# Retention outputs copied out of PSUM at once, and a planner that counts series of narrow matmuls

## The chip, the cores and the metric

The kernel runs on one core of one Trainium2 chip. The metric is the device time of one execution in microseconds (us); the kernel before is given by the median of three runs. Profiles are of single executions.

## The reference

The program is a two-layer decoder trunk on 1024 positions of width 1024, all in float32. Layer 0 is a retention layer with 4 heads (query/key width 256, value width 512), layer 1 a stick-breaking attention with 8 heads. The change touches the retention layer's output and the order of the whole program. Cut to what matters:

```python
u = rms_norm(h, ret_norm_pre); proj = u @ ret_w_in            # q, k, v, g
q, k = rope(q), rope(k) * 256 ** -0.5
o = retention_chunkwise(q, k, v)                              # per head: (q k^T * decay) v + state
mu  = mean(o, axis=-1); var = mean((o - mu) ** 2, axis=-1)    # over a head's 512 values
o = (o - mu) * rsqrt(var + EPS)                               # normalise each row of each head
o = merge_heads(o) * silu(g)
y = o @ ret_w_out; h = h + rms_norm(y, ret_norm_post)
... # shared K/V from h, then layer 1: stick-breaking attention with its own q and gate
A[t,s] = sigmoid(z_ts) * prod_{s<j<t} (1 - sigmoid(z_tj));  o = A v;  y = (o * silu(g)) @ sb_w_out
h = h + rms_norm(y, sb_norm_post)
```

## The kernel before

**How the work is tiled.** Positions come in two halves of 512, each in blocks of 128 (one block is the 128 partitions). Every float32 product is made of three matmuls, since each operand is kept as a high and a low part (`split`: ScalarE (ACT) copies the source rounded to the matmul's type, then VectorE (DVE) subtracts it from the source for the low part). A matmul with 512 moving columns is called wide here; one with 384, 256 or 128 columns, and every 128x128 transpose by an identity matrix, is narrow. The large projections (weights `wraw`/`raw` loaded from memory, split into `whl`; input parts `xh`, `qk`, `oT`, `op`) use two-by-two block products with seven instead of eight block multiplications, so sums of weight blocks are formed on DVE first. They accumulate in the PSUM banks `pma` and `pmb` (two each), and in part in `pz` and `po`.

**Stages.** First the retention layer's projections (to about 430 us). Then, spread between further projections, the eight retention units (4 heads by 2 halves, about 430 to 690 us): scores in `pz` (two banks), outputs in `po` (two banks). Then the first output projection, normalisation and the second layer's projections, the stick-breaking heads (about 1100 to 1500 us: score rows in `pz`, a scan on DVE, transposes of the weights `A` into `pz`, split into `AT`, products into `po`), and the last projection.

**One retention block.** `o(ib)` in `AHead.mix` computes a block's 128x512 output in a `po` bank. DVE takes its mean and variance from the bank (`bn_stats`, `bn_aggr`, and the negated mean `nm`), GpSimd (POOL) adds epsilon, raises to the power -1/2 and multiplies (`r`, `nb`). One call later `normed()` has ACT read the bank once more, with scale `r` and bias `nb`, into the SBUF tile `on` (a half of a `sgn` buffer); in `gate()` DVE multiplies by the gate `sg` and PE transposes the four 128x128 pieces into `pz`, from where ACT copies them to `on`/`o` for storage. Bank `po` is held until that second reading.

**What sets the order.** All operations are recorded first (`Recorder`), with their dependencies through tiles: a reader depends on the writers of the same cells and a writer on their readers, while two readers do not depend on each other. `Plan` then orders every engine's queue. `Plan.run` walks a clock forward with the costs from `Recorder.cost`: for PE it looks at the next 100 matmuls in program order and takes the one with the lowest sum of lateness (its operand should be ready EARLY = 350 ns ahead), expected waiting (times IDLE = 10) and distance from the front (PLACE = 5 ns each). The other engines take, of what is ready first, what is due first (`Plan.limits`). Ten rounds are made, each with the due times of the last, and each resulting order is tried with random durations (`Plan.trial`, six tosses); the order with the lowest mean is emitted. Loads and stores are issued by SyncE (SP) in an order set the same way. Instructions are recorded at one line of the file (L234, L235 after the change), so the profile tells them apart by tile names: `po<-v,sc` writes a tile `po` from `v` and `sc`.

In this kernel's rope step, which comes up below, DVE forms four products from two PSUM banks and a table (`f<-po,tab`), and POOL adds them in pairs (`f<-f,f`).

Of the kernel before, what the change touches and what calls it, by code (L numbers as in the profile page):

```python
# [45 lines left out]
EARLY, PLACE, IDLE = 350, 5, 10  # L46
# [99 lines left out]
class Recorder:  # L146
# [39 lines left out]
    def cost(self, o, out, ins):  # L186
# [9 lines left out]
        if e == PEE:  # L196
            fp = ins[0].tile.dt == F32 and m == "transpose"
            if m == "transpose":
                pace = 111 if fp else 58 + (0 if self.turning else 142)
            else:  # L200
                pace = max(13.3 + n / 2.4, 112) + (2 if n == 512 else 0)
            self.turning = m == "transpose" and not fp
            o.step, o.took = pace, pace + 162
            return
# [82 lines left out]
class Plan:  # L287
# [39 lines left out]
    def run(self, late, look=True):  # L327
# [16 lines left out]
        since = {}  # L344
# [20 lines left out]
        def best(e):  # L365
            if e == PEE:
                c = None
                for k, i in enumerate(pe[:PE_AHEAD]):
                    if c and k * PLACE >= c[0]:
                        break  # L370
                    if need[i]:
                        continue
                    r = possible(i)
                    if r is None:
                        continue
                    x = max(r if r > ready[i] else 0.0, given[i])
                    wait = max(r - free[e], 0.0)
                    x = max(x + EARLY - free[e], 0.0) + wait * IDLE + k * PLACE
                    if c is None or x < c[0]:
                        c = (x, free[e] + wait, i)  # L380
# [20 lines left out]
        while len(order) < n:  # L401
# [13 lines left out]
            else:  # L415
                took = o.took
                if o.port:
# [32 lines left out]
    def trial(self, order, seed):  # L450
# [3 lines left out]
        busy, server = {DVEE: 0.0, POOLE: 0.0}, 0.0  # L454
# [3 lines left out]
        for o in order:  # L458
# [14 lines left out]
            elif e == PEE:  # L473
                more = 0 if o.step < 200 or x > 0.16 else 6.5 if x > 0.01 else 90
# [42 lines left out]
def trunk(ctx, tc, xT, wts, gains, trig, ident_in, cols, grow_in, out):  # L517
# [299 lines left out]
    class AHead:  # L817
# [65 lines left out]
        def mix(self):  # L883
# [40 lines left out]
            def o(ib):  # L924
# [10 lines left out]
                for jb in blocks:  # L935
                    n = slice(128 * (ib - jb), 128 * (ib - jb) + 128)
                    sc, v = self.sc[jb], self.v[jb]
                    mm3(p[:], sc[:, 0, n], sc[:, 1, n], v[:, 0, :], v[:, 1, :], not state and jb == first, jb == ib)
                bs, mv = S("small", [6]), S("small", [2])
# [8 lines left out]
                late.append((ib, p, r, nb))  # L948
# [5 lines left out]
            def normed():  # L954
                ib, p, r, nb = late.pop(0)
                if ib % 2 == 0:
                    self.on2 = S("sgn", [1024])
                on = self.on2[:, 512 * (ib % 2):512 * (ib % 2) + 512]
                A_.activation(on, p[:], AF.Identity, scale=r[:], bias=nb[:])
                self.on.append(on)  # L960
# [842 lines left out]
```

## Time and profile before

| what | value |
| --- | --- |
| median of three runs | 1577.93 us (1577.35 to 1577.95) |
| the profiled execution | 1576.62 us, its span 1574.9 us |
| PE busy | 1565.2 us (99%), 7416 matmuls |
| DVE busy | 1304.8 us (83%) |
| ACT busy | 828.3 us (53%) |
| POOL busy | 212.6 us (13%) |
| mean granted TensorE clock | 0.999 |

The profile's page gives busy times by engine, groups of instructions (line, engine, operation, `out<-in` by tile names, shapes, count, busy time, mean duration of one, idle time before them and what ended it), and the chain of work that ended last. The trace also answers with the waits of one engine, with a timeline of one engine in a window (start in us, time covered in us, instruction, count; consecutive instructions of one kind are one row), and with busy times by window. Matmuls overlap in the pipeline, so that a duration of 389 ns goes with a start every 227 ns: pace is read from starts.

### The profile page before, as it was taken

The page shows a single profiled execution, that of the slowest core. Times are in us where ns is not written, and L with a number is a line of the kernel's source. Part 1 is how long each engine was busy: PE and PEld are TensorE (multiplying, and loading weights), DVE is VectorE, ACT ScalarE, POOL GpSimd, SP SyncE. Part 2 cuts the span into 40 slices and gives each one's busy share as a digit, 9 for nine tenths or more (in the row PEclk, how much of TensorE's full clock was granted, in tenths as well). Part 3 has the DMA queues.
Part 4 walks back from the last instruction along what each step waited for, and adds up shares of the span by engine and source line. Part 5 has one row for each costly group of instructions (what it writes and reads, how often), then busy time and mean ns, then how long its engine had stood idle before and what let it go on. Part 6 is the DMA issues. An engine that isn't in the chain of part 4 may idle for free.

```text
span 1574.9 us, 22257 instructions
## 1 busy us (share of the span) xinstructions
PE 1565.2 (99%) x7416; PEld 1305.7 (83%) x7416; DVE 1304.8 (83%) x1909; ACT 828.3 (53%) x1470; POOL 212.6 (13%) x298
## 2 busy tenths in 40 slices
PE   9999999999999999999999999999999999999998
PEld 7888888878888888888888888888888888888886
DVE  7999889797677988999989856748788878777888
ACT  7643432313466765646665545545555655554564
POOL 0100015240022222420000000001120111211100
PEclk9999999999999999999999999999999999999999
DMA  8779887378556897884686969667889768884674
GB/s 293 250 256 333 282 324 236 128 258 291 177 189 215 303 342 272 318 312 164 219 295 239 327 212 348 223 238 260 298 303 347 255 239 298 312 324 156 231 282 170
DMA packets 176946, 414.20 MB, mean 263 GB/s; under 512 B 19904, under 2 KB 20544, under 8 KB 176832
## 3 DMA queue, kind: packets, MB, share of 16 engines
q1 hardware_dynamic: 176688, 412.73, 74.0%
q8 instruction: 58, 0.95, 0.2%
q14 instruction: 56, 0.46, 0.1%
q10 hardware_dynamic: 144, 0.07, 0.0%
HBM read 299.47 MB, written 113.25 MB: 262 GB/s over the span
## 4 chain that ended last, share of the span: by engine, by line
PE 99%; DVE 1%; issue 0%; POOL 0%; ACT 0%; DVEq 0%; ACTq 0%
PE pma L234 29%; PE pmb L234 29%; PE po L234 23%; PE pz L234 19%; POOL col L234 0%; DVE whl L234 0%; DVE wraw L234 0%; DVE f L234 0%; DVE small L234 0%; DVE A L234 0%; DVE S L234 0%; ACT f L234 0%; DVEq L1799 0%; ACT acc L234 0%; ACT AT L234 0%
## 5 line engine op out<-in xcount | busy, mean ns | idle before, releaser
L234 ACT ACTIVATE whl<-wraw 128x512 fp32r<-128x512 f32 (+1 forms) x264 | 157.8, 628 | 240.8 <-DVE wraw L234 69.6
L234 DVE TENSOR_TENSOR whl<-wraw,whl 128x512 fp32r<-128x512 f32 x264 | 187.5, 733 | 77.2 <-ACT whl L234 76.7
L234 PE MATMUL pma<-whl,xh 128*128 128x512 f32 x480 | 126.4, 393 | 1.2 <-DVE whl L234 1.0
L234 PE MATMUL pmb<-whl,xh 128*128 128x512 f32 x480 | 124.3, 390 | 0.0
L234 PE MATMUL pmb<-xh,whl 128*128 128x512 f32 x408 | 105.9, 390 | 0.0
L234 PEld LDWEIGHTS pmb<-whl,xh 128*128 128x128 f32 x480 | 89.6, 188 | 18.6 <-ACT f L234 0.3
L234 PE MATMUL pma<-xh,whl 128*128 128x512 f32 x408 | 105.0, 390 | 0.0
L234 PEld LDWEIGHTS pma<-whl,xh 128*128 128x128 f32 x480 | 88.5, 188 | 19.0 <-DVE whl L234 1.5
L234 PE MATMUL pz<-ko,ko 128*128 128x384 f32 (+3 forms) x480 | 95.8, 323 | 0.0
L234 ACT ACTIVATE AT<-pz 128x512 fp32r<-128x512 f32 (+2 forms) x96 | 44.6, 490 | 97.2 <-PE pz L234 96.0
L234 PE MATMUL pma<-op,whl 128*128 128x512 f32 x336 | 89.8, 396 | 0.0
L234 PEld LDWEIGHTS pmb<-xh,whl 128*128 128x128 f32 x408 | 76.4, 188 | 15.6
L234 PEld LDWEIGHTS pma<-xh,whl 128*128 128x128 f32 x408 | 76.2, 188 | 15.6
L234 POOL TENSOR_TENSOR f<-f,f 128x512 f32<-128x512 f32 x32 | 54.3, 1705 | 249.1 <-DMA raw<-in_wts_dram 153.4
L234 PE MATMUL pmb<-op,whl 128*128 128x512 f32 x336 | 87.6, 391 | 0.0
L234 PEld LDWEIGHTS pz<-ko,ko 128*128 128x128 f32 x480 | 77.8, 189 | 9.4
L234 DVE SCALAR_TENSOR_TENSOR wraw<-wraw,gn,wraw 128x512 f32<-128x512 f32 x96 | 70.7, 747 | 17.7 <-ACT wraw L234 11.8
L234 POOL TENSOR_SCALAR_AFFINE_SELECT f<-f 128x128 f32<-128x128 f32 x64 | 28.9, 469 | 405.5 <-DMA g<-sg 286.6
L234 DVE TENSOR_TENSOR_SCAN sgn<-sgn 128x640 f32<-128x640 f32 (+3 forms) x32 | 61.8, 1932 | 21.8 <-POOL sgn L234 21.7
L234 PE MATMUL pz<-xh,whl 128*128 128x512 f32 x312 | 79.4, 389 | 0.0
L234 PE MATMUL po<-xh,whl 128*128 128x512 f32 x312 | 79.2, 389 | 0.0
L234 DVE TENSOR_TENSOR AT<-pz,AT 128x512 fp32r<-128x512 f32 (+2 forms) x96 | 51.0, 551 | 33.0 <-ACT AT L234 32.9
(220 smaller groups left out, 3682.6 us busy)
## 6 DMA issues: line engine op xcount, KB each, us to landing
wraw<-in_wts_dram SPq DMA_DIRECT2D x431, 256.0 KB, 5.2
raw<-in_wts_dram SPq DMA_DIRECT2D x64, 512.0 KB, 7.1
v<-v SPq DMA_DIRECT2D x64, 512.0 KB, 5.7
ko<-kq SPq DMA_DIRECT2D x40, 512.0 KB, 6.0
raw<-o SPq DMA_DIRECT2D x36, 512.0 KB, 6.6
raw<-oc SPq DMA_DIRECT2D x36, 512.0 KB, 6.6
kq<-v SPq DMA_DIRECT2D x32, 512.0 KB, 6.5
s<-f SPq DMA_DIRECT2D x40, 256.0 KB, 3.4
```

Source lines behind the costliest of these rows:

```text
L234: f(*[_real(a) for a in o.args], **{k: _real(v) for k, v in o.kw.items()})
```

## The change

It has two parts.

1. In `o(ib)` ACT copies the bank into the `sgn` buffer as soon as the block's last matmul is done (`AF.Copy`); `bn_stats` still reads the bank; `normed()` then normalises in place in SBUF. The `sgn` buffer is therefore taken in `o(ib)` instead of in `normed()`.
2. The planner marks narrow PE operations. In `Plan.run` a wide matmul after a narrow one is charged TURN = 300 ns in the choice, so that a series of narrow ones is continued where one is to be had; a narrow one after a wide one moves the plan's clock by SERIES = 40 ns. In `Plan.trial` that charge takes the place of random extra times on wide matmuls; the 2 ns extra for 512 columns in `cost` is dropped.

```diff
--- before.py
+++ after.py
@@ -43,7 +43,7 @@
 DMA_TIME = 4000.0
 PE_AHEAD = 100
 FILL = 15000.0
-EARLY, PLACE, IDLE = 350, 5, 10
+EARLY, PLACE, IDLE, TURN, SERIES = 350, 5, 10, 300, 40
 ROUNDS, TRIALS = 10, 6
 
 
@@ -195,10 +195,11 @@
             return
         if e == PEE:
             fp = ins[0].tile.dt == F32 and m == "transpose"
+            o.narrow = n < 512
             if m == "transpose":
                 pace = 111 if fp else 58 + (0 if self.turning else 142)
             else:
-                pace = max(13.3 + n / 2.4, 112) + (2 if n == 512 else 0)
+                pace = max(13.3 + n / 2.4, 112)
             self.turning = m == "transpose" and not fp
             o.step, o.took = pace, pace + 162
             return
@@ -341,7 +342,7 @@
         ahead = {tag: list(seq) for tag, seq in self.turn.items()}
         left = {t: len(u) for t, u in self.users.items()}
         last = dict.fromkeys(self.users, 0.0)
-        since = {}
+        since, narrow = {}, False
         for o in ops:
             if not need[o.i] and o.engine != PEE:
                 waiting[o.engine].append(o.i)
@@ -375,7 +376,7 @@
                         continue
                     x = max(r if r > ready[i] else 0.0, given[i])
                     wait = max(r - free[e], 0.0)
-                    x = max(x + EARLY - free[e], 0.0) + wait * IDLE + k * PLACE
+                    x = max(x + EARLY - free[e], 0.0) + wait * IDLE + k * PLACE + (TURN if narrow and not ops[i].narrow else 0)
                     if c is None or x < c[0]:
                         c = (x, free[e] + wait, i)
                 return c and c[1:]
@@ -414,6 +415,10 @@
                 free[e] = t + o.step
             else:
                 took = o.took
+                if e == PEE:
+                    if o.narrow and not narrow:
+                        t += SERIES
+                    narrow = o.narrow
                 if o.port:
                     other = POOLE if e == DVEE else DVEE
                     if port[other] > t:
@@ -451,7 +456,7 @@
         toss = random.Random(seed)
         ops = self.ops
         end, after, free = [0.0] * len(ops), [0.0] * len(ops), [0.0] * 5
-        busy, server = {DVEE: 0.0, POOLE: 0.0}, 0.0
+        narrow, busy, server = False, {DVEE: 0.0, POOLE: 0.0}, 0.0
         slots = {tag: [0.0] * seq[0].bufs for tag, seq in self.turn.items()}
         left = {t: len(u) for t, u in self.users.items()}
         since, last = {}, dict.fromkeys(self.users, 0.0)
@@ -471,7 +476,8 @@
                 end[i] = server + (217 if o.store else 717) + toss.expovariate(1 / 250)
                 free[e] = t + 430
             elif e == PEE:
-                more = 0 if o.step < 200 or x > 0.16 else 6.5 if x > 0.01 else 90
+                more = SERIES if o.narrow and not narrow else 0
+                narrow = o.narrow
                 end[i] = t + o.took + more
                 free[e] = t + o.step + more
             else:
@@ -936,6 +942,10 @@
                     n = slice(128 * (ib - jb), 128 * (ib - jb) + 128)
                     sc, v = self.sc[jb], self.v[jb]
                     mm3(p[:], sc[:, 0, n], sc[:, 1, n], v[:, 0, :], v[:, 1, :], not state and jb == first, jb == ib)
+                if ib % 2 == 0:
+                    self.on2 = S("sgn", [1024])
+                on = self.on2[:, 512 * (ib % 2):512 * (ib % 2) + 512]
+                A_.activation(on, p[:], AF.Copy)
                 bs, mv = S("small", [6]), S("small", [2])
                 V.bn_stats(bs[:], p[:])
                 V.bn_aggr(mv[:], bs[:])
@@ -945,18 +955,15 @@
                 G.tensor_tensor(r[:], mv[:, 1:2], cc[:, 16 + 4 * h + ib:17 + 4 * h + ib], ALU.add)
                 G.tensor_tensor(r[:], r[:], mhalf[:, 0:1], ALU.pow)
                 G.tensor_tensor(nb[:], nm[:], r[:], ALU.mult)
-                late.append((ib, p, r, nb))
+                late.append((on, r, nb))
                 if ib:
                     normed()
 
             late = []
 
             def normed():
-                ib, p, r, nb = late.pop(0)
-                if ib % 2 == 0:
-                    self.on2 = S("sgn", [1024])
-                on = self.on2[:, 512 * (ib % 2):512 * (ib % 2) + 512]
-                A_.activation(on, p[:], AF.Identity, scale=r[:], bias=nb[:])
+                on, r, nb = late.pop(0)
+                A_.activation(on, on, AF.Identity, scale=r[:], bias=nb[:])
                 self.on.append(on)
 
             def first():
```

Since the planner orders the whole program, every engine's order changes. Counted in PE's order, the 1192 narrow matmuls and transposes stood in 238 unbroken series, and stand in 168 now. Three places follow.

**DVE near 347 us of the profile before**, where `whl542` (weights of the projection that accumulates in `pma538` to `pmb541`) gets its second low half, the last row. Before:

```order
L234 TENSOR_TENSOR wraw547_3430<-wraw546_3418,wraw547_3430 128x512
L234 TENSOR_TENSOR f2529_3500<-po426_2760,tab228_1408 128x512
L234 TENSOR_TENSOR wraw548_3438<-wraw548_3438,wraw547_3430 128x512
L234 TENSOR_TENSOR f2530_3512<-po427_2765,tab227_1400 128x512
L234 TENSOR_TENSOR wraw551_3458<-wraw550_3446,wraw551_3458 128x512
L234 TENSOR_TENSOR whl542_3456<-wraw548_3438,whl542_3456 128x512
```

Now:

```order
L235 TENSOR_TENSOR wraw547_3431<-wraw546_3419,wraw547_3431 128x512
L235 TENSOR_TENSOR wraw548_3440<-wraw548_3440,wraw547_3431 128x512
L235 TENSOR_TENSOR wraw551_3459<-wraw550_3448,wraw551_3459 128x512
L235 TENSOR_TENSOR whl542_3457<-wraw548_3440,whl542_3457 128x512
L235 TENSOR_TENSOR wraw552_3467<-wraw552_3467,wraw551_3459 128x512
L235 TENSOR_TENSOR f2529_3525<-po426_2756,tab228_1410 128x512
```

The two rope products `f2529` and `f2530` stood ahead of the low half of `whl542` and now stand behind it.

**PE in the stick-breaking stage**, where two tiles of transposed weights (`pz2214`, `pz2217`) are finished and the first of them, split into `AT2215`, is multiplied into `po2222`. Before:

```order
L234 MATMUL pz2214_12188<-ident_68,A2200_12160 128x128
L234 MATMUL pz2217_12191<-ident_68,A2200_12160 128x128
L234 MATMUL pmb2135_11769<-oT1607_8629,whl2208_12148 128x512 x2
L234 MATMUL pmb2136_11775<-oT1607_8629,whl2208_12148 128x512 x2
L234 MATMUL po2222_12245<-AT2215_12234,vo2213_12072 128x512
```

Now:

```order
L235 MATMUL pmb2136_11814<-oT1607_8666,whl2208_12199 128x512 x3
L235 MATMUL pz2214_12215<-ident_68,A2200_12193 128x128
L235 MATMUL pz2217_12221<-ident_68,A2200_12193 128x128
L235 MATMUL po2222_12277<-AT2215_12272,vo2213_12108 128x512
L235 MATMUL po2223_12281<-AT2215_12272,vo2213_12108 128x512
L235 MATMUL pz2220_12285<-ident_68,A2171_12002 128x128
```

Between the end of `pz2214` and the product that needs its split there stood one transpose and four wide matmuls, and now stands one transpose. In another head (`pz2732`, `AT2733`) it is the other way round: there one transpose and one wide matmul stood between them, and now one transpose and four wide matmuls.

**PE in a retention unit**, from a block's last matmuls (`po798` before, `po799` now) to the last transposes of its normalised output (`pz816`). Before:

```order
L234 MATMUL po798_4739<-v762_4617,sc2739_4570 128x512 x3
L234 MATMUL pz807_4773<-ident_68,sgn784_4661 128x128 x4
L234 MATMUL pz808_4780<-ko741_4407,ko745_4425 128x256 x3
L234 MATMUL pz808_4780<-ko743_4413,ko747_4436 128x256 x3
...
L234 MATMUL pz815_4834<-ident_68,sgn805_4742 128x128 x4
L234 MATMUL pma830_4840<-whl797_4321,qk143_1035 128x512 x3
L234 MATMUL pma831_4847<-whl797_4321,qk143_1035 128x512
L234 MATMUL pz816_4851<-ident_68,sgn805_4742 128x128 x4
```

Now:

```order
L235 MATMUL po799_4747<-v762_4598,sc2739_4587 128x512 x3
L235 MATMUL pz807_4780<-ident_68,sgn765_4607 128x128 x4
L235 MATMUL pz808_4788<-ko741_4414,ko745_4435 128x256 x3
L235 MATMUL pz808_4788<-ko743_4422,ko747_4466 128x256 x3
...
L235 MATMUL pz815_4841<-ident_68,sgn787_4719 128x128 x4
L235 MATMUL pma830_4848<-whl798_4332,qk143_1036 128x512 x3
L235 MATMUL pz816_4854<-ident_68,sgn787_4719 128x128 x4
```

(In the gap marked "..." stand 12 wide matmuls and the 4 transposes of `pz814` in both.) One wide matmul fewer stands between the block's end and its last transposes. In DVE's order of the changed program the statistics of 29 of the 32 blocks wait for ACT's copy of the same bank, and in the other 3 the copy waits for the statistics: the framework that builds the program puts the two readings of one bank one after the other, which the planner's dependencies don't hold. With the waits shown, DVE has for this block:

```order
L235 BN_STATS small801_4784<-po799_4747 128x6 [waits Activation_49]
L235 BN_AGGR small802_4795<-small801_4784 128x2 [waits DVE_49]
```

and before:

```order
L234 BN_STATS small800_4776<-po798_4739 128x6 [waits PE_49]
```

Here the wait is for ACT instead of for PE.

## The prediction

> **What bounds the kernel now.** I read the page's busy times and chain first, then PE's own waits, then PE's timeline at the places that those waits name.
>
> ```profile
> PE 1565.2 (99%) x7416; PEld 1305.7 (83%) x7416; DVE 1304.8 (83%) x1909; ACT 828.3 (53%) x1470; POOL 212.6 (13%) x298
> PE 99%; DVE 1%; issue 0%; POOL 0%; ACT 0%; DVEq 0%; ACTq 0%
> ```
>
> PE is the bound from end to end: 99% of the span is its work, and 99% of the chain that ended last. The number of matmuls does not change. So the change can only take away time in which PE stands still or goes slower than it could, and it can only cost what makes PE wait. PE's waits, all of them:
>
> ```profile
> PE pz L234 <- DVE onesr L234: 1.4, 1, 1.4
> PE pma L234 <- DVE whl L234: 1.0, 1, 1.0
> PE po L234 <- ACT AT L234: 0.3, 1, 0.3
> PE pz L234 <- POOL col L234: 0.2, 1, 0.2
> ```
>
> The first is the program's start. None of the others is a wait for a `po` bank: the bank that the first part of the change frees earlier was never missed. What can be won is the second and third wait, and small change. (A wait in this list is only the gap after the pipeline has run dry; the time lost is read from starts below.)
>
> **The pace, and what a series costs.** The first term rests on PE's timeline (start, time covered, instruction, count):
>
> ```profile
> 471.78 1.52 PE L234 MATMUL pmb<-whl,xh 128*128 128x512 f32 x6
> 473.14 1.52 PE L234 MATMUL po<-ko,ko 128*128 128x512 f32 x6
> ...
> 480.43 1.03 PE L234 MATMUL pz<-ident,sgn 128*128 128x128 f32 x8
> 481.22 1.17 PE L234 MATMUL pma<-whl,qk 128*128 128x512 f32 x4
> 482.23 0.60 PE L234 MATMUL pz<-ident,sgn 128*128 128x128 f32 x4
> ...
> 1482.68 0.38 PE L234 MATMUL pz<-ident,A 128*128 128x128 f32 x2
> 1482.82 1.17 PE L234 MATMUL pmb<-whl,op 128*128 128x512 f32 x4
> 1483.83 0.38 PE L234 MATMUL pz<-ident,A 128*128 128x128 f32 x2
> ```
>
> Six wide matmuls take 473.14 - 471.78 = 1.36, so 0.2267 each. From 480.43 to 482.23 are 8 transposes and 4 wide matmuls, 1.80; from 1482.68 to 1483.83 are 2 and 4, 1.15. The difference gives 0.65 / 6 = 0.108 for a transpose, and 1.15 - 0.907 - 0.217 = 0.026 is left for going into a series and out again. Starts are given to 0.01 and a wide matmul is sometimes a few ns late, so a series costs between 0 and 0.04; I take 0.02, below the reading because it holds such lateness too. The orders have 238 and 168 series: 70 fewer x 0.02 = **-1.4 us** (0 to -2.8).
>
> **The wait near 349 us.** Four engines around it, PE first, then DVE, ACT, POOL:
>
> ```profile
> 347.93 0.61 PE L234 MATMUL pz<-whl,qk 128*128 128x512 f32 x2
> 348.68 0.72 PE L234 MATMUL pma<-whl,xh 128*128 128x512 f32 x2
> 349.25 0.63 PE L234 MATMUL pmb<-whl,xh 128*128 128x512 f32 x2
> 350.90 1.19 PE L234 MATMUL pma<-whl,xh 128*128 128x512 f32 x4 [1.03 <-DVE whl L234]
> 351.93 1.07 PE L234 MATMUL pmb<-whl,xh 128*128 128x512 f32 x4
> ```
>
> ```profile
> 346.68 0.69 DVE L234 TENSOR_TENSOR f<-po,tab 128x512 f32<-128x512 f32 x1
> 347.28 0.68 DVE L234 TENSOR_TENSOR wraw<-wraw,wraw 128x512 f32<-128x512 f32 x1
> 347.88 0.68 DVE L234 TENSOR_TENSOR f<-po,tab 128x512 f32<-128x512 f32 x1
> 348.48 0.68 DVE L234 TENSOR_TENSOR wraw<-wraw,wraw 128x512 f32<-128x512 f32 x1
> 349.08 1.77 DVE L234 TENSOR_TENSOR whl<-wraw,whl 128x512 fp32r<-128x512 f32 x1
> ...
> 348.00 0.63 ACT L234 ACTIVATE whl<-wraw 128x512 fp32r<-128x512 f32 x1 [0.57 <-DVE wraw L234]
> ...
> 348.69 1.60 POOL L234 TENSOR_TENSOR f<-f,f 128x512 f32<-128x512 f32 x1 [6.93 <-ACT whl L234]
> ```
>
> From 347.93 to 351.93 are 4.00 us for 10 wide matmuls, which need 2.27: 1.73 lost. PE first wants the high half (ACT, done 348.63), then the low one (DVE, done 350.85, stretched from 0.68 to 1.77 while POOL works until 350.29). In the new order the two `f<-po,tab` stand behind. Then the second sum starts at 346.68 instead of 347.28, ACT's copy runs from 347.40 to 348.03, and the low half from about 348.07 to 348.75; POOL's step waits for one of the moved products and begins after it. Without its first wait (0.30) PE asks for the high half at 348.38 and, four matmuls on, for the low one near 349.29. Both are there, with 0.35 and 0.5 to spare: **-1.7 us** (0 if that margin is eaten by a later start of DVE, which a moved transfer could bring).
>
> **The wait near 1485 us goes, and comes back elsewhere.**
>
> ```profile
> 1483.96 0.48 PE L234 MATMUL pmb<-whl,op 128*128 128x512 f32 x1
> 1484.78 0.73 PE L234 MATMUL po<-AT,vo 128*128 128x512 f32 x2 [0.34 <-ACT AT L234]
> 1485.51 0.66 PE L234 MATMUL pz<-ident,A 128*128 128x128 f32 x4
> 1485.92 1.17 PE L234 MATMUL po<-AT,vo 128*128 128x512 f32 x4
> 1486.93 0.60 PE L234 MATMUL pz<-ident,A 128*128 128x128 f32 x4
> ```
>
> From 1483.83 to 1486.93 are 3.10 us for 6 transposes and 7 wide matmuls in two series: 0.65 + 1.59 + 0.04, so 0.82 lost. One transpose and one wide matmul (0.34) stand there between the finished tile and the product that needs its split. Now four wide matmuls do, and the 0.82 goes. But at `AT2215` only the one transpose (0.11) is left: the same chain with 0.23 less cover, 0.82 + 0.23 = 1.05. Together **+0.2 us** (-0.8 to +0.4).
>
> **The copy, and the bank read twice.** Rows of several views: the timeline of one block's chain; the group of ACT's plain copies out of `po`; the three POOL steps (min/median/max in ns, first and last start); and the retention stage by engine (PE, PEld, DVE, ACT, POOL busy).
>
> ```profile
> 476.75 0.70 DVE L234 BATCH_NORM_STATS2 small<-po 128x6 f32<-128x512 f32 x1 [0.36 <-PE po L234]
> 479.08 0.78 ACT L234 ACTIVATE sgn<-po,small,small 128x512 f32<-128x512 f32 x1
> 479.89 0.69 DVE L234 TENSOR_TENSOR sgn<-sgn,sg 128x512 f32<-128x512 f32 x1
> ...
> L234 ACT ACTIVATE f<-po 128x512 f32<-128x512 f32 x28 | 16.6, 594 | 8.4 <-PE po L234 7.7
> ...
> L234 POOL TENSOR_TENSOR small<-small,cc x32: 189/366/1152, 432.3 to 684.4; 128x1 f32<-128x1 f32 x32
> L234 POOL TENSOR_TENSOR small<-small,mhalf x32: 548/879/2080, 432.6 to 685.5; 128x1 f32<-128x1 f32 x32
> L234 POOL TENSOR_TENSOR small<-small,small x32: 185/192/1899, 433.5 to 687.1; 128x1 f32<-128x1 f32 x32
> 430.00:690.00 260.00, 260.00 (x1294) 218.83 (x1293) 222.67 (x364) 159.38 (x262) 81.26 (x125) 1.00 0.76 276
> ```
>
> The new work is 32 such copies, 0.594 each: 19 us on ACT, busy 159 of 260. Normalising now reads SBUF; the ACT copy from SBUF above took 0.63 against 0.594 from PSUM, so I add 0.03 to 0.78. That alone would be hidden. But the statistics of 29 blocks now wait for ACT's copy of the same bank. No row of before has ACT and DVE at one `po` bank at the same time, so what they would do without the order is not seen here; with it, the chain grows by the copy, a hop and the slower normalising, about 0.65.
>
> The Trainium skill says in "PSUM — Partial Sum Buffer", section "PSUM bank collisions raise a hardware error", that two engines must not be at one bank in the same partitions together, two readers included, and that the chip doesn't arbitrate. By that rule the order is needed and the 0.65 stays on the chain; were the two readings free to overlap, the copy term below would be 0 and the sum -2.9. No run here shows a collision.
>
> What hides the 0.65? From the statistics' start to the end of DVE's multiplication the chain took 480.58 - 476.75 = 3.83, with POOL at its fastest (0.19 + 0.55 + 0.19). With POOL's medians (1.44 in all) it is 4.34, and 4.99 with the addition. The order leaves, between `po799` and `pz816`, 12 transposes, 6 matmuls of 256 columns (0.12 each, between the two paces) and 15 wide ones: 1.30 + 0.72 + 3.40 = 5.42, where it was 5.65. That holds by 0.4 less two hops, and fails when POOL is slow: its maxima add up to 5.1 instead of 1.44. Counted in the order, a second place has 6.3 us of cover; all others have over 9. So two places can show the whole copy: 2 x 0.59 = **+1.2 us**. Below, it is 0. Above: DVE stands at the statistics until the copy is done, and all that is queued behind it (splits of weights, of values, of the state) comes later. DVE is idle 37 us of the stage, and 32 x 0.65 = 21 fits into it, so as a sum it is covered; if one block in each of the eight units found it uncovered, it would be 8 x 0.65 = 5.2.
>
> **The sum.** -1.4 - 1.7 + 0.2 + 1.2 = -1.7 us. The durations are from an execution of 1576.62 us with a span of 1574.9, 1.3 below the median of the three runs; I take the difference over to the median: 1577.93 - 1.7 = 1576.2. About 0.2%, 3.2 us, is what a measurement of this kernel can tell from no change.
>
> **Rivals.** (1) *Joining series saves nothing, and only waits are traded.* The 0.026 read above is two or three times the rounding of the starts, and part of it is late wide matmuls. Then the sum is -0.3: 1577.6. The freed bank was not waited for, so the first part does nothing for PE in this case either. Against it: both windows give the same sign.
>
> The Trainium skill's "TensorE: Matmul & The Clock Gate", section "LDWEIGHTS (loading the stationary operand)", gives 128 columns / 1.2 = 107 ns for a load of weights, whatever stood before. By that rule a narrow matmul is paced by its own weights, a series has no price, and this rival's 1577.6 follows; the trace's 0.108 for a transpose agrees with it.
>
> (2) *A series costs what the planner now charges, 0.04, and the copy is covered everywhere.* 70 x 0.04 = 2.8, so -2.8 - 1.7 + 0.2 = -4.3: 1573.6. For it: it is within the rounding of the first window. Against: the second window's 0.026 already holds the jitter.
>
> (3) *Slower: DVE, held at the statistics by a copy that stands in ACT's queue, hands its splits over late.* The place is the retention stage, where DVE is busy 223 of 260 and would be held up to 21 us more. Price 0.65 for each block that isn't covered. From ten such blocks on (6.5 - 2.9 = +3.6) it decides; with two in each unit it is 16 x 0.65 = 10.4, 1585.4. For it: the planner does not know of this wait, so nothing was put there to cover it. Against: 30 of 32 blocks have over 9 us of cover for their own chain.
>
> **How the numbers follow.** Forecast 1576.2 with 0.45, (1) 0.27, (2) 0.17, (3) 0.11. Faster by over 0.2% needs 1574.8 or less: (2), less a little of it, and a little of the forecast's lower tail: 0.17. Slower needs 1581.1 or more: (3), 0.11. The rest, 0.72, is the same. The range runs from 1574.0, which leaves out the lower half of (2), to 1580.0, which leaves out (3); the forecast's own range is 1575.0 to 1577.6.
>
> **What would show it.** Right: no wait of PE for `whl` near 349 us; none near 1485, but one of about 1 us for ACT `AT` near 1232; in the retention stage short PE waits for `sgn` in `pz`, about 1 us in all, near 480 first; DVE's idle time before its statistics now ended by ACT. The series: the span shorter by more than these waits explain. Wrong: if the wait for `whl` is still there, the margins worked out at 349 were too thin; if PE's waits in the retention stage come to several us, it is (3); if the waits are as forecast and the time is still 1577.6, it is (1).

## The result, and the profile after

The changed kernel takes 1575.42 us (median of 22 executions, 1574.24 to 1576.71), the kernel before, beside it, 1577.89 (22 executions, 1576.26 to 1579.09). The ratio is 0.9986, with a 95% interval from 0.998 to 0.9991: 2.2 us less, between 1.4 and 3.2, and so inside the 0.2% called no change. The forecast was 1576.2.

The two profiled executions do not show this difference: 1576.62 before and 1576.69 after, spans 1574.9 and 1575.0. The first lies at the fast end of its kernel's executions, the second at the slow end of its own. So the places are compared one by one, over several profiles. PE's busy time and the chain on the page of after, and PE's waits (us in total, times, longest):

```profile
PE 1564.9 (99%) x7416; PEld 1307.4 (83%) x7416; DVE 1302.2 (83%) x1909; ACT 846.3 (54%) x1502; POOL 225.1 (14%) x298
PE 96%; DMA 1%; DVE 1%; ACT 1%; issue 0%; SPq 0%; DVEq 0%; ACTq 0%
```

```profile
PE pz L235 <- DVE onesr L235: 1.4, 1, 1.4
PE po L235 <- ACT AT L235: 0.6, 1, 0.6
PE po L235 <- ACT v L235: 0.6, 1, 0.6
PE pmb L235 <- ACT f L235: 0.4, 1, 0.4
PE pz L235 <- DMA ko<-kq: 0.2, 1, 0.2
```

The wait for `whl` is gone and a longer one for `AT` is there, as forecast. No wait is for `sgn`; in the retention stage PE waits for `v` and for a bank that ACT empties (`f`). DVE, ACT and PE near 349 us, in the timelines of after:

```profile
346.15 2.01 DVE L235 TENSOR_TENSOR wraw<-wraw,wraw 128x512 f32<-128x512 f32 x3
348.25 0.69 DVE L235 TENSOR_TENSOR whl<-wraw,whl 128x512 fp32r<-128x512 f32 x1
348.86 0.68 DVE L235 TENSOR_TENSOR wraw<-wraw,wraw 128x512 f32<-128x512 f32 x1
349.46 1.28 DVE L235 TENSOR_TENSOR f<-po,tab 128x512 f32<-128x512 f32 x2
350.66 0.68 DVE L235 TENSOR_TENSOR whl<-wraw,whl 128x512 fp32r<-128x512 f32 x1
...
354.28 0.63 ACT L235 ACTIVATE whl<-wraw 128x512 fp32r<-128x512 f32 x1 [3.98 <-DVE wraw L235]
...
349.36 1.07 PE L235 MATMUL pma<-whl,xh 128*128 128x512 f32 x4
350.27 1.07 PE L235 MATMUL pmb<-whl,xh 128*128 128x512 f32 x4
...
353.90 1.33 PE L235 MATMUL pz<-whl,qk 128*128 128x512 f32 x5
355.06 0.62 PE L235 MATMUL pma<-whl,xh 128*128 128x512 f32 x2
```

The low half runs from 348.25 to 348.94, forecast 348.07 to 348.75, and PE starts on it at 349.36 without a gap, 0.42 later. The high half, ACT's copy, ends at 348.22, 0.23 before PE starts on it at 348.45. The rows from 350.66 on matter below. Near 1232 us PE has:

```profile
1232.35 0.38 PE L235 MATMUL pz<-ident,A 128*128 128x128 f32 x2
1233.36 0.73 PE L235 MATMUL po<-AT,vo 128*128 128x512 f32 x2 [0.64 <-ACT AT L235]
```

The groups of DVE's statistics and ACT's normalising (busy time, mean ns | idle time before them, and what ended it):

```profile
L235 DVE BATCH_NORM_STATS2 small<-po 128x6 f32<-128x512 f32 x32 | 22.3, 698 | 19.2 <-ACT sgn L235 17.3 <-PE po L235 2.0
L235 ACT ACTIVATE sgn<-sgn,small,small 128x512 f32<-128x512 f32 x32 | 25.9, 811 | 10.9 <-POOL small L235 10.8
```

DVE stands 17.3 us at its statistics for ACT's copy, as the built order says.

### The profile page after: what moved, and what is told of

The parts are those of the page before. It is cut to its first block, busy times and chain, and to the rows that moved or that the text cites. A ratio compares the mean times of both kernels' runs of the same rounds, so it can differ in the third digit from the quotient of the medians.

```text
span 1575.0 us, 22320 instructions
## 1 busy us (share of the span) xinstructions
PE 1564.9 (99%) x7416; PEld 1307.4 (83%) x7416; DVE 1302.2 (83%) x1909; ACT 846.3 (54%) x1502; POOL 225.1 (14%) x298
## 4 chain that ended last, share of the span: by engine, by line
PE 96%; DMA 1%; DVE 1%; ACT 1%; issue 0%; SPq 0%; DVEq 0%; ACTq 0%
PE pma L235 28%; PE pmb L235 28%; PE po L235 22%; PE pz L235 18%; DMA ko<-kq 0%; DMA f<-st 0%; DMA f<-av 0%; DMA st<-f 0%; DVE small L235 0%; DVE f L235 0%; ACT sgn L235 0%; ACT v L235 0%; DVE ko L235 0%; ACT whl L235 0%; DVE v L235 0%
## 5 line engine op out<-in xcount | busy, mean ns | idle before, releaser
L235 DVE TENSOR_TENSOR whl<-wraw,whl 128x512 fp32r<-128x512 f32 x264 | 184.1, 720 | 78.5 <-ACT whl L235 77.4
L235 POOL TENSOR_SCALAR_AFFINE_SELECT f<-f 128x128 f32<-128x128 f32 x64 | 32.9, 524 | 400.1 <-DMA g<-sg 284.6
L235 PE MATMUL pma<-whl,op 128*128 128x512 f32 x288 | 77.4, 397 | 0.0
```

The lines of the kernel that those rows point to most:

```text
L235: f(*[_real(a) for a in o.args], **{k: _real(v) for k, v in o.kw.items()})
```

## A table of lost time

All profiles of this study can be laid over each other. For each matmul the distance from the end before it to its own end is taken, less its pace (0.227, 0.175, 0.119 and 0.112 us for 512, 384, 256 and 128 columns, 0.109 for a float32 transpose: medians of these traces; 0.080 for a transpose of rounded values, whose median is 0.084). What is over 0.09 at one matmul is counted at its place; the small remainders of the other 7400 are the column "rest". Span less all lost time is 1563.8 to 1564.0 in every one of the twelve profiles: that is all matmuls at their pace and the program's two ends, so the table holds all of the differences between the spans (us):

| kernel | series | start (0-12) | 300-365 | 430-690 | 690-800 | 1100-1300 | 1480-1576 | other | rest | span |
| --- | --- | --- | --- | --- | --- | --- | --- | --- | --- | --- |
| before | 238 | 2.00 | 1.71 | 0 | 0 | 0 | 0.83 | 0.47 | 6.04 | 1574.9 |
| e3 | 238 | 2.02 | 1.69 | 0.92 | 0 | 0 | 0.82 | 0 | 6.23 | 1575.6 |
| e3b | 238 | 2.88 | 2.27 | 0.35 | 0 | 0 | 0.82 | 0.38 | 6.26 | 1577.0 |
| e2 | 229 | 1.99 | 0.79 | 2.06 | 0 | 1.13 | 0 | 0 | 6.40 | 1576.2 |
| e1 | 171 | 2.18 | 1.81 | 0 | 1.69 | 1.21 | 0.70 | 0 | 4.64 | 1576.1 |
| after | 168 | 2.53 | 0 | 2.60 | 0 | 1.56 | 0 | 0 | 4.40 | 1575.0 |
| after again (a2) | 168 | 3.49 | 0 | 2.12 | 0 | 1.22 | 0 | 0 | 4.68 | 1575.4 |
| e4 | 168 | 2.04 | 0 | 1.86 | 0 | 1.74 | 0 | 0 | 4.63 | 1574.1 |
| e5 | 172 | 2.02 | 0 | 0.20 | 1.20 | 1.12 | 0 | 0 | 4.37 | 1572.8 |
| e6 | 168 | 2.17 | 0 | 0.70 | 0 | 0.52 | 0 | 0 | 4.76 | 1572.0 |
| e8 | 168 | 3.34 | 1.69 | 1.07 | 0 | 1.56 | 0 | 0 | 4.75 | 1576.3 |
| e9 | 168 | 3.00 | 1.18 | 1.60 | 0 | 1.21 | 0 | 0 | 4.38 | 1575.2 |

The labels are those of the experiments below. "Series" counts the unbroken series of narrow operations, "other" is 12 to 300 and 365 to 430 us. The column to begin with is "rest". It is 6.04 to 6.40 with the old planner and 4.37 to 4.76 with the new one, and by place it stands at the series: the first narrow operation of a series and the first seven wide matmuls behind it carry 6.29 to 6.52 us in the four old orders and 4.30 to 4.55 in the eight new ones, 0.025 to 0.028 for each series in all twelve. (Of this saving of 2.0 us, 0.4 comes back elsewhere, most of it between the operations of the now longer series.)

## The experiments

**One part of the change alone.** e1 has the new planner and normalises out of the bank as before; e2 has the old planner and the copy.

```diff
# e1, against the changed kernel
-                A_.activation(on, p[:], AF.Copy)
-                late.append((on, r, nb))
+                late.append((ib, p, r, nb))
-                A_.activation(on, on, AF.Identity, scale=r[:], bias=nb[:])
+                A_.activation(on, p[:], AF.Identity, scale=r[:], bias=nb[:])
```

> The new planner (TURN, SERIES) with the old normalisation, which reads the po bank a second time and holds it; 171 series against 238. My theory (a series costs about 0.02, the copy costs about 1.2 us and brings nothing): 67 fewer series give -1.3, and whatever PE waits this order has are read off its own wait list; with the two waits of before (1.7 near 349 and 0.8 near 1485) also gone 1574.2 to 1575.0. Rival A (a series costs nothing, each plan only trades waits for other waits): 1577 to 1578, the wait list sets it. Rival B (the copy itself is what helps, by freeing the bank early): above the changed kernel's 1575.4 and near 1577.9, with PE waits for po banks.

> The old planner with the copy out of the bank; 229 series against 238 of the kernel before. My theory: the copy brings nothing and costs 0 to 2.6 us of PE waits in the retention stage (430 to 690 us), series -0.2: 1577.7 to 1580, with DVE's statistics waiting for ACT's copies. Rival B (the copy itself helps): 1575.4 to 1576.5.

Measured beside 1577.47 of before: e1 1578.68, ratio 1.0005 [0.9996, 1.0014]; e2 1577.95, 1.0002 [0.9993, 1.0011]. Neither part alone gains; together they gave 0.9986. But each of the three is a plan with waits of its own. PE's waits of e1:

```profile
PE pma L235 <- ACT whl L235: 1.1, 2, 0.7
PE po L235 <- ACT AT L235: 0.6, 1, 0.6
PE pmb L235 <- DVE S L235: 0.5, 1, 0.5
PE po L235 <- DVE AT L235: 0.4, 1, 0.4
```

No wait of e1 is for a `po` bank, so rival B falls. e1's rest is 4.64 against 6.04 of before, as my theory asks; but its plan has 1.81 lost between 346 and 355 us, 1.69 near 760, and two waits for `AT`, 1.12 near 1234 and 0.70 near 1495. My theory's 1574.2 to 1575.0 held only if the two old waits went and nothing came in their place, and that was not so. e2 keeps the rest (6.40) and loses 2.06 in the retention stage, within its forecast.

**The wait near 349 us.** e3 does on the kernel before what my prediction took for the cause, and nothing else (POOL's addition of the two products moves with them).

```diff
# e3: before's order, DVE
 wraw547
-f2529 (rope product)
 wraw548
-f2530 (rope product)
 wraw551
 whl542 (low half)
+f2529
+f2530
```

> The kernel before in its own order; only the two rope products (f from po and tab) near 346.7 and 347.9 us, with POOL's addition of them, are moved on DVE right behind the low half of the weights tile that PE waits for near 349 us. My theory: this wait (1.7 us) goes and nothing replaces it: 1576.2. Rival A (DVE has no slack there, so that the lateness goes to the next weights tile, a few us later): 1577.9, with a PE wait for whl of about 1 us between 350 and 357 us.

Measured: 1577.93, ratio 1.0003 [0.9994, 1.0012]. Rival A holds. e3's timelines of DVE and PE:

```profile
347.81 0.69 DVE L234 TENSOR_TENSOR whl<-wraw,whl 128x512 fp32r<-128x512 f32 x1
348.42 1.28 DVE L234 TENSOR_TENSOR f<-po,tab 128x512 f32<-128x512 f32 x2
...
351.91 0.68 DVE L234 TENSOR_TENSOR f<-po,tab 128x512 f32<-128x512 f32 x1
352.51 0.68 DVE L234 TENSOR_TENSOR whl<-wraw,whl 128x512 fp32r<-128x512 f32 x1
...
353.24 1.19 PE L234 MATMUL pma<-whl,xh 128*128 128x512 f32 x4 [0.93 <-DVE whl L234]
```

`whl542` is in time, but the two products now stand ahead of the next weights tile, `whl549`; its low half is ready at 353.19, and 1.69 is lost again, 2 us later. In the changed kernel that half runs at 350.66, ahead of a weight sum and of the third product. So e3b takes over that whole stretch of DVE's order:

```diff
# e3b: before's order, DVE, behind whl542
+wraw552, f2529, f2530, whl549 (first low half), wraw554, whl560, wraw555, f2527, whl549, f2528, whl560
-wraw552, wraw554, f2527, whl549, wraw555, f2528, whl549, ..., whl560, whl560
```

> The kernel before in its own order; on DVE the whole stretch from the weight sums near 346 us to the split of whl560 stands in the changed kernel's order: the two rope products behind, and besides them the first low half of the next weights tile whl549 ahead of a weight sum and of the third product. My theory now (the products behind move the wait to whl549, and it goes only because that tile's split is drawn forward too): 1576.2, with PE's waits between 346 and 358 us at 0.3 or less. Rival (DVE has too much to do there and the wait goes further, to the next tile): 1577.5 to 1578, with 1 us or more of waits for whl there.

Measured beside 1577.97 of before: 1579.03, ratio 1.0005 [0.9996, 1.0014]: my theory fell again. ACT and PE of e3b:

```profile
355.12 0.63 ACT L234 ACTIVATE whl<-wraw 128x512 fp32r<-128x512 f32 x1 [3.98 <-DVE wraw L234]
...
355.80 0.74 PE L234 MATMUL pma<-whl,xh 128*128 128x512 f32 x2 [0.84 <-ACT whl L234]
```

Now PE reaches the second half of `whl549` before ACT has copied it (355.75). In the changed kernel five wide matmuls on a tile already split (`pz<-whl,qk` at 353.90, 1.16 us) stand there, and ACT's copy ends at 354.91 for a need at 355.06. (Of the 2.27 that e3b lost from 300 to 365 us, 1.12 is this wait. Another 1.00 is lost at 361.6, where PE waits for a `pmb` bank; ACT empties it late, behind a split that stood 1.18 for its load of weights.) Two undo experiments in the changed kernel test both parts:

```diff
# e8: the changed kernel's order, DVE          # e9: the changed kernel's order, PE
 wraw547                                        pmb <- whl549 (first half)
+f2529                                         -pz576, pz577 <- whl560,qk (5 wide)
 wraw548                                        pma, pmb <- whl549 (second half, 12 wide)
+f2530                                         +pz576, pz577 <- whl560,qk
 wraw551                                        po578, po579 <- whl560,qk
 whl542
```

> The changed kernel in its own order; only the two rope products near 349.5 us are put back on DVE where they stood before, between the three weight sums. My theory: the low half of whl542 is late again, since the products stand ahead of it and POOL's addition runs beside it: +1.7, 1577.1, with a PE wait for whl of about 1 us near 350. Rival (what went at 349 us is not due to the products, but to transfers or PE's order): 1575.4.

> The changed kernel in its own order; only five wide matmuls (whl560 with qk) that stand on PE near 354 us between the two products of the tile whl549 are put behind them, where the kernel before had them still later. My theory now (the wait near 349 us stays away because three engines' orders changed together, and these five cover ACT's copy of whl549's second half): PE asks for that half at 353.9, ACT has it at 354.95, so a wait of about 1.0 near 354 and 1576.4, 1.0 above the changed kernel. Rival (moving the two rope products on DVE is enough by itself): no wait there, 1575.4.

Measured: e8 1577.55 beside 1577.97 of before, 0.9994 [0.9985, 1.0003]; e9 1576.82 beside 1577.95, 0.9991 [0.9982, 1.0]. Against the unchanged a2 (1575.27, beside the same runs of before as e8) e8 is 2.3 us slower; 1.69 of this is the wait. DVE, POOL and PE of e8, then ACT and PE of e9:

```profile
350.11 1.77 DVE L235 TENSOR_TENSOR whl<-wraw,whl 128x512 fp32r<-128x512 f32 x1
...
349.73 1.60 POOL L235 TENSOR_TENSOR f<-f,f 128x512 f32<-128x512 f32 x1 [6.93 <-ACT whl L235]
...
351.94 1.19 PE L235 MATMUL pma<-whl,xh 128*128 128x512 f32 x4 [1.02 <-DVE whl L235]
```

```profile
354.84 0.63 ACT L235 ACTIVATE whl<-wraw 128x512 fp32r<-128x512 f32 x1 [3.98 <-DVE wraw L235]
...
355.52 0.73 PE L235 MATMUL pma<-whl,xh 128*128 128x512 f32 x2 [0.91 <-ACT whl L235]
```

Each undo brings its wait back where it was expected: 1.69 lost in e8, forecast 1.7, and 1.18 in e9, forecast 1.0. (e9's interval overlaps that of the changed kernel, so that its loss is shown by the place and not by the time.) The 1.7 us at this place need the two products behind (e8), the next tile's split ahead of them on DVE (e3), and five matmuls drawn forward on PE (e9). Whether these three are enough in the old order was not tried.

**The order on the bank.** e4 turns it round; e5 takes the statistics from the copy and plans anew.

```diff
# e4: the changed kernel's order, in 26 blocks      # e5: the changed kernel
-copy (ACT), bn_stats (DVE) waits for it            -                V.bn_stats(bs[:], p[:])
+bn_stats (DVE), copy (ACT) waits for it            +                V.bn_stats(bs[:], on)
```

> The changed kernel in its own order on every engine; only which reader of the po bank has to wait for the other is turned round in 26 blocks: ACT's copy now waits for DVE's statistics instead of the statistics for the copy. My theory (the order on the bank holds DVE up and makes its splits late, about 2.6 us of PE time in 430 to 690 us, of which 1.0 to 2.4 come back): 1573.0 to 1574.4, DVE idle before the statistics ended by ACT near 0 instead of 17.3 us. Rival (the lateness in that stage comes from elsewhere, POOL's slow steps or the gathered order): 1575.4, with the same short waits for v, sc and f.

> The changed kernel with one line different: the statistics read the SBUF copy instead of the po bank, and the order is planned anew with this dependency known to the planner (172 series). My theory (the planner did not know that the statistics wait for the copy; now it does and places covers accordingly): the short waits in 430 to 690 us shrink from about 2.6 to 1.0 or less, 1573.5 to 1574.5. Rival (a new plan only trades waits for others): 1575 to 1577, and the wait list names them.

Measured: e4 1576.14 beside 1577.47, 0.9992 [0.9983, 1.0001]; e5 1574.83 beside 1577.45, 0.9985 [0.9976, 0.9994]. The groups of e4:

```profile
L235 DVE BATCH_NORM_STATS2 small<-po 128x6 f32<-128x512 f32 x32 | 22.3, 695 | 8.7 <-PE po L235 6.4 <-POOL small L235 1.0 <-POOL sc L235 0.6
L235 ACT ACTIVATE sgn<-po 128x512 f32<-128x512 f32 x32 | 19.1, 598 | 49.0 <-DVE small L235 49.0
```

DVE's wait is gone, and the time is no better: ACT stands 49.0 us at its copies, all for DVE, where it stood 32.4 in the changed kernel, nearly all for PE, and the retention stage still loses 1.86. My theory falls as a sum; one place did get better, as shown below. e5 loses 0.20 there, as its theory asks, but its new plan has 1.20 at 765 us (a transpose waits for `acc`), and its gain over before is that of the changed kernel, its 1574.83 between the two forecasts. That is what the rival said of a new plan.

**The cover near 1232 us.**

```diff
# e6: the changed kernel's order, PE
 pmb2136 (3 wide)
+pz2214, pz2217 (transposes of A)
 pmb2136 (3 wide)
-pz2214, pz2217
 po2222 <- AT2215
```

> The changed kernel in its own order; only two transposes of A are moved ahead of three wide matmuls near 1231 us, so that three wide matmuls and one transpose stand between the finished A tile and the product that needs its split, instead of one transpose. My theory (the loss there, 1.1 us by starts, is cover that is missing, 0.68 of it is given back): 1574.7, with PE's wait for AT there 0 to 0.1 instead of 0.64. Rival (ACT or DVE is late for another reason and the wait stays): 1575.4.

Measured: 1574.11 beside 1577.45, ratio 0.9981 [0.9972, 0.999]: 3.3 us below before, 0.9 more than the changed kernel gained. PE of e6:

```profile
1229.39 0.38 PE L235 MATMUL pz<-ident,A 128*128 128x128 f32 x2
1229.52 0.94 PE L235 MATMUL pmb<-oT,whl 128*128 128x512 f32 x3
1230.40 0.73 PE L235 MATMUL po<-AT,vo 128*128 128x512 f32 x2
```

No wait is left; by ends 0.43 is lost here instead of 1.12. The 0.69 difference is the 0.68 forecast. e6 has the lowest median of the study; its interval and those of the changed kernel (0.9986, and 0.9983 when run again) overlap, so that it is faster than that kernel is shown by the place and not by the times alone.

**The price of a series, by itself.** Two kernels of constant matmuls.

```diff
# s1: 96 narrow and 96 wide in a phase          # s2: 24 series in a phase, six wide after each
+for kind in "fmrn":                            +for kind in "fmrn":
+    for length in (2, 4, 8, 16):               +    for length in (1, 2, 4, 8):
+        for _ in range(96 // length):          +        for _ in range(24):
+            length x narrow(kind)              +            length x narrow(kind)
+            length x wide()                    +            six()
```

> Leaves out all of the kernel's computation: it only issues narrow and wide matmuls on constant tiles and writes zeros. Four kinds of narrow operation (float32 transposes, 128-column matmuls, fp32r transposes, 256-column matmuls) alternate with wide ones, 96 narrow and 96 wide in a phase, in series of 2, 4, 8 and 16. The slope of a phase's duration over its number of series (48, 24, 12, 6) is the price of a series. My theory: 0.02 us for each. Rival A (a narrow matmul is paced by its own weights load, series cost nothing): the four phases of a kind are equally long to 0.2 us. Rival B (the planner's 0.04): 48 series are 1.7 us longer than 6.

> Leaves out all of the kernel's computation: only matmuls on constant tiles, zeros as output. 24 series of 1, 2, 4 and 8 narrow operations of one kind, each series followed by the same six wide matmuls that accumulate in one bank; four kinds (float32 transposes, 128 columns, fp32r transposes, 256 columns). The time of a phase over the length of its series is a line: its slope is the pace of a narrow operation, what it has at length 0 above six wide matmuls is the price of a series. My theory: 0.02 on average, more for transposes (0.03 to 0.04) than for narrow matmuls (0.01 to 0.02). Rival A: 0 for every kind. Rival B: 0.04 for every kind.

s1's phases took, for series of 4, 8 and 16: float32 transposes 32.85, 32.60, 32.46 us; 128 columns 32.80, 32.97, 32.82; fp32r transposes 31.04, 30.62, 30.36; 256 columns 33.68, 33.52, 33.40. From 24 to 6 series that is 0.022, 0, 0.038 and 0.016 for each. But the 128-column phases go up and down by 0.17, and the phase of 48 series of two took 33.44 for 256 columns, less than that of 24 series. In s1 short series also have few wide matmuls between them, so it decides nothing. s2 is cleaner. First and last series of four of its phases, 20 cycles apart in the first and 23 in the others:

```profile
59.14 0.27 PE L78 MATMUL pza<-ident,raw 128*128 128x128 f32 x1
...
89.08 0.27 PE L78 MATMUL pza<-ident,raw 128*128 128x128 f32 x1
...
173.20 1.03 PE L78 MATMUL pza<-ident,raw 128*128 128x128 f32 x8
...
225.30 1.03 PE L78 MATMUL pza<-ident,raw 128*128 128x128 f32 x8
...
400.14 0.22 PE L80 MATMUL pzb<-identr,w 128*128 128x128 f32 x1
...
434.57 0.22 PE L80 MATMUL pzb<-identr,w 128*128 128x128 f32 x1
...
516.10 0.80 PE L80 MATMUL pzb<-identr,w 128*128 128x128 f32 x8
...
564.29 0.80 PE L80 MATMUL pzb<-identr,w 128*128 128x128 f32 x8
```

A cycle of one float32 transpose and six wide matmuls is 29.94 / 20 = 1.497, one of eight 52.10 / 23 = 2.265: 0.110 for a transpose, and 1.497 - 1.360 - 0.110 = 0.027 for the series. For fp32r transposes it is 0.085 and 0.051. A line through all four lengths gives 0.030 for float32 transposes, 0.018 for 128 columns, 0.051 for fp32r transposes and 0.032 for 256 columns. Rival A (nothing) is out, and so is rival B (0.04 for all): three kinds lie below, one above. My theory has float32 transposes and 128 columns right; fp32r transposes and 256 columns cost 0.01 more than the most it gave them.

The Trainium skill's "TensorE: Matmul & The Clock Gate", section "LDWEIGHTS (loading the stationary operand)", gives a load of weights P / 1.2 ns, where P is its columns, so 107 ns for 128. The 0.110 of a float32 transpose agrees with it as a pace, the 0.085 of an fp32r transpose lies below it, and the measurement decides. The rule has no term for a series, and s2 shows one.

**The changed kernel once more.**

> The changed kernel, unchanged, profiled and timed once more beside the others. Theory A (the short waits of its first profile in the retention stage, 2.6 us in 430 to 690 us, belong to that execution: most of them go back to a load of the state that landed late): another execution shows 0.4 to 1.2 us there, and the median is again 1575.4, 2.5 below the kernel before. Theory B (they are what the copy and the new order cost in every execution): about 2.6 us at the same places.

Measured: 1575.27 beside 1577.97, 0.9983 [0.9974, 0.9992]: the result stands. The retention stage lost 2.12, nearer to theory B. But with the same order there, e6 lost 0.70, e8 1.07 and e9 1.60. What differs is a transfer. ACT's row near 454 us in a2, and in e6:

```profile
455.33 0.63 ACT L235 ACTIVATE ko<-f 128x512 fp32r<-128x512 f32 x1 [0.94 <-DMA f<-st]
```

```profile
453.11 0.62 ACT L235 ACTIVATE ko<-f 128x512 fp32r<-128x512 f32 x1
```

In a2 ACT stands at this split of the state until its load has landed, and the copy that empties a `pmb` bank stands behind it; in e6 the load is there. The split stood 1.15, 0.94, 0.60, 0.51, 0.29 and 0 us for its load in after, a2, e9, e8, e4 and e6, and PE lost 0.84, 0.64, 0.37, 0.17, 0 and 0 near 456 to 459. So both theories hold in part: a share comes in every execution, a share only when the state lands late.

## Why the prediction was right, and where it was not

**The series** (-1.4, by 0.02 for each). Right, a little small. Over the table, the rest is 6.04 to 6.40 with the old planner (mean 6.23 of four, 236 series) and 4.37 to 4.76 with the new one (mean 4.58 of eight, 169 series): -1.65 us, 0.025 for a series, and no overlap. This term is in every kernel of the new planner, e1 too, and it stands where the series end. Rival (1), by which joining series saves nothing, falls.

**The wait near 349** (-1.7). Right in size and place, and wrong in its reason. With the two products behind, the halves were there, with 0.23 and 0.42 to spare where 0.35 and 0.5 were forecast; but the prediction did not ask which tile is late next. e3 shows that the step as I argued it gains nothing. The changed plan gains because it moved two more things on two other engines, which my working did not look at.

**The `AT` waits** (+0.2). Right: 0.83 near 1485 gone, 1.12 near 1232 (forecast 1.05), +0.29 in all. e6 shows that it was cover, as counted in the order.

**The copy** (+1.2). The mean comes near the size; the places were other ones, and in part the mechanism. Orders that normalise out of the bank lost 0, 0, 0.35 and 0.92 in the retention stage (before, e1, e3b, e3; mean 0.32). Those with the copy beside the statistics lost 0.70 to 2.60 (after, a2, e2, e6, e8, e9; mean 1.69): about +1.4. But nothing was lost at `pz816`: its chain from ACT's copy at 476.21 to the end of DVE's multiplication took 4.55, where 4.99 was forecast for POOL's medians (POOL was at its fastest here), and the transposes came at 481.46. What all five executions of the changed order (after, a2, e6, e8, e9) lose stands at three other places, 0.7 to 0.9 us together.

The first is rival (3)'s. DVE, ACT and PE of after:

```profile
460.00 0.70 DVE L235 BATCH_NORM_STATS2 small<-po 128x6 f32<-128x512 f32 x1 [1.00 <-ACT sgn L235]
...
465.16 0.63 ACT L235 ACTIVATE ko<-f 128x512 fp32r<-128x512 f32 x1 [2.24 <-DVE f L235]
...
465.31 1.99 PE L235 MATMUL po<-ko,ko 128*128 128x512 f32 x6
```

DVE stands 1.00 at the statistics for a copy that stands behind splits in ACT's queue, and is then busy without a pause until the state's sum `f` ends at 465.13. ACT splits that sum, and the second of PE's six matmuls starts only at 465.84, when the split is done: 0.41 lost, and 0.20 to 0.41 in the other four. In e4, where the statistics come first, nothing is lost here.

The second is near 488. ACT and PE of after:

```profile
487.05 0.60 ACT L235 ACTIVATE sgn<-po 128x512 f32<-128x512 f32 x1 [0.64 <-DVE small L235]
487.54 0.71 ACT L235 ACTIVATE v<-f,ncc 128x512 fp32r<-128x512 f32 x1
...
487.70 0.96 PE L235 MATMUL po<-v,vo 128*128 128x512 f32 x3
```

This is one of the three blocks where the copy waits for the statistics. PE's next product into a `po` bank starts at 487.70, 0.05 after the copy has ended, and while the split of `v` that stands behind the copy still runs (to 488.25). So it is the bank that PE waits for: it comes free only when both readings are done, one after the other, and 0.38 is lost. The same 0.38 or 0.39 stands there in a2, e4, e6, e8 and e9, each time 0.05 after the copy; e5, whose statistics don't read the bank, loses nothing there. The prediction held from the waits of before that no `po` bank was ever missed; with two readers in a row one is. The third place, a `pz` bank that ACT empties near 539, costs 0.13 to 0.15.

What after and a2 lost beyond this stands behind late loads: 0.84 and 0.64 near 456 to 459, as shown above, and at splits of `v` 0.84 near 516 in after and 0.60 near 491 in a2. e3's 0.45 and 0.11 near 491, in the old order, stand behind a load too. So of the 1.4 between the means 0.7 to 0.9 is there in every execution, at three places instead of ten, and the first two of these are made by the order of the bank's two readings. Whether the copies' 19 us on ACT have a part in the rest is open.

**The sum.** -1.65 - 1.7 + 0.3 + 1.4 = -1.65 against -1.7 forecast, and -1.4 to -3.2 measured (medians: -2.5, and -2.7 for a2). The terms' agreement with the median is partly luck: the profile that the sum was made against had lost nothing in the retention stage, and other executions of nearly the same order (e3, e3b) lost 0.92 and 0.35 there, so that part of the +1.4 is in executions of before as well.

## What to carry to other kernels

When a wait is to be removed by moving work behind the late operation, follow the moved work to the next operation that must be on time, on each engine, until a real gap takes it up; here the lateness went round three engines before it did. When a second reader of a bank is added, ask when the bank comes free if the readings come one after the other. A new plan from a search is a new set of small waits: price what all of its orders share (here 0.025 us for each series) apart from the waits of one order, and over several profiles. What one order leaves can then be mended by hand at one place, as in e6.

## What the runs showed of the hardware

**A series of narrow matmuls has a price that depends on its kind**: in s2, with six wide matmuls behind each series, 0.018 us for 128 columns, 0.030 for float32 transposes, 0.032 for 256 columns and 0.051 for fp32r transposes, on top of a pace of 0.085 to 0.118 for each operation. In the twelve traces of the program it is 0.025 to 0.028, spread over the first seven wide matmuls behind.

**A VectorE operation was stretched past the end of a GpSimd operation that had begun before it.** In e8 POOL's addition runs from 349.73 to 351.33, and DVE's `whl`, begun at 350.11, takes 1.77 instead of 0.69 and ends 0.55 after it. The Trainium skill's "SBUF — State Buffer", section "SBUF: two separate sides", says that these two engines share a pair of ports as an exclusive lock for the whole instruction, when the VectorE operation has two inputs in SBUF; the trace agrees. In the changed kernel the lengthened operation is a weight sum that nobody waits for yet.

**Executions of one order differ here mostly by where loads land.** After and a2, one kernel, differ by 0.96 us in the first 12 us, by what they lose behind loads in the retention stage, and by 0.35 near 1159, where after waits for a load. In all twelve profiles the first 12 us lose 2.0 to 3.5. In a2 the third piece of the input is there at 7.94, in e6 at 6.68 (ACT's rows):

```profile
7.94 0.72 ACT L235 ACTIVATE oT<-S,gn 128x512 fp32r<-128x512 f32 x1 [1.93 <-DMA S<-in_xT_dram]
```

```profile
6.68 0.72 ACT L235 ACTIVATE oT<-S,gn 128x512 fp32r<-128x512 f32 x1 [0.56 <-DMA S<-in_xT_dram]
```

PE stands 1.23 us in a2 for the split behind that row. Such a difference in one profile is as large as half of what the change brought.
